# Log-softmax over 8192 rows: which 32 rows make up a tile, and what that does to the shape of its transfers

## The chip, the cores and the metric

The kernel runs on one core of a Trainium2 chip. The metric is device microseconds (us) of one execution. Three runs of the kernel before took 7587.55, 7586.4 and 7587.37 us, median 7587.37 us.

## The reference

The input is float32 of shape 16 x 512 x 50000, that is 8192 rows of 50,000 numbers (200,000 bytes a row, 1638.4 MB in all). The output has the same shape.

```python
max_x = np.max(x, axis=-1, keepdims=True)
shifted = x - max_x
log_sum_exp = np.log(np.sum(np.exp(shifted), axis=-1, keepdims=True))
return (shifted - log_sum_exp).astype(np.float32)
```

Each row is independent of every other one, so the rows may be taken in any order and any grouping.

## The kernel before, in words

**Tiles.** A tile is 32 rows (`R`). Each row is cut into four parts (`G`), so that a tile fills 128 partitions with 12,500 numbers (50,000 bytes) each. There are 256 tiles (`ntiles`) and four buffers (`NBUF`), and tile t lives in buffer t modulo 4. A buffer is loaded, worked on in place and stored; then it is loaded again.

**Which rows.** `halves` (L77 to L79) views the array as two halves of 128 tiles. Tile t is tile t // 2 of half t % 2, so that even tiles come from the first 4096 rows and odd ones from the last 4096. The 32 rows of a tile are neighbours in memory: the 128 partitions read 128 neighbouring stretches of 50,000 bytes. `run` (L85 to L94) gives the same tiles to the loops, where the tile number is in a register.

**The first tile** is taken in four pieces (`NS`), so that work starts as soon as a quarter of it is there. A piece is eight whole rows, each cut into 16 parts (`GS`) of 3,125 numbers (12,500 bytes), one to a partition. `xs` and `os` (L82, L83) are the views for it. Pieces are loaded at L173 and stored from `in_parts` of the scalar engine through L278. The last tile is stored in four pieces too, but these are quarters of the columns of an ordinary tile (L334).

**Engines.** SP issues the loads (L170 whole tiles, L173 the pieces of the first tile); before a buffer is loaded again, SP waits until its store has landed (`take`, L49). ACT issues the stores (L278). The two queues are called q10 and q1 in the profile. DVE takes the maxima of four column blocks of a tile (L231), agrees them among the four partitions of a row, and at the end subtracts maximum and logarithm in place over the whole tile (L219). ACT takes the exponentials (L286) as the maxima come, and the logarithm (L274). PE adds up the partial sums of a row with a small matmul (L340). ACT issues the store of tile t - 1 when it is half through the exponentials of tile t (`GATE`).

**Order.** Everything is written out by hand with semaphores: SP loads pieces 0 to 3 of tile 0, then tiles 1, 2, 3, and then each further tile as soon as the store of the tile four before it has landed. A loop of 63 rounds of four tiles makes up the middle.

Of the kernel before, what the change touches and what calls it, by code (L numbers as in the profile page):

```python
# [16 lines left out]
G = 4  # L17
R = P // G
C = 3125
NBUF = 4  # L20

NS = 4

GATE = 2
GS = G * NS
RS = P // GS
# [20 lines left out]
def take(engine, sem, n=16):  # L47

    engine.wait_ge(sem, n).then_inc(sem, -n)  # L49


def cols(c):
    return slice(c * C, (c + 1) * C)
# [3 lines left out]
def kernel(  # L57
# [6 lines left out]
    xf = x.flatten_outer_dims()  # L64
    of = out.flatten_outer_dims()
# [3 lines left out]
    ntiles = N // R  # L69


    rounds = (ntiles - NBUF) // NBUF
# [1 line left out]
    tail = range(1 + rounds * NBUF, ntiles)  # L74


    def halves(a):  # L77
        both = a.rearrange("(h t r) (g w) -> h t (r g) w", h=2, r=R, g=G)
        return [both[t % 2, t // 2] for t in range(ntiles)], both  # L79

    (xt, xh), (ot, oh) = halves(xf), halves(of)
    xs = xf.rearrange("(t s r) (g w) -> t s (r g) w", s=NS, r=RS, g=GS)  # L82
    os = of.rearrange("(t s r) (g w) -> t s (r g) w", s=NS, r=RS, g=GS)  # L83

    def run(both, first, n):  # L85

        k = NBUF // 2

        def tile_of(q, i):
            h, t = (first + i) % 2, (first + i) // 2  # L90
            part = both[h, t : t + k * (n - 1) + 1 : k]
            return part[bass.ds(q, 1)].rearrange("o p w -> (o p) w")

        return tile_of  # L94

    data = ctx.enter_context(tc.tile_pool(name="data", bufs=1))
    stats = ctx.enter_context(tc.tile_pool(name="stats", bufs=1))
# [10 lines left out]
    bufs = [data.tile([P, W], FP32, name=f"buf{j}") for j in range(NBUF)]  # L108
# [41 lines left out]
    @block.gpsimd  # L150
    def _(gpsimd):
        k = 0
        for g in (GS, G):
            view = ones[g].rearrange("p (r g) -> p r g", g=g)
            r = P // g
            gpsimd.memset(ones[g], 1.0).then_inc(ready)
            gpsimd.affine_select(  # L157
                out=view, in_=view, pattern=[[-g, r], [0, g]], base=0,
                channel_multiplier=1, compare_op=ALU.is_ge, fill=0.0,
            ).wait_op(ready, k + 1, "sem-ge").then_inc(ready)  # L160
            gpsimd.affine_select(  # L161
                out=view, in_=view, pattern=[[g, r], [0, g]], base=g - 1,
                channel_multiplier=-1, compare_op=ALU.is_ge, fill=0.0,
            ).wait_op(ready, k + 2, "sem-ge").then_inc(ready)
            k += 3

    @block.sync
    def _(sync):
        def load(j, src):
            sync.dma_start(out=bufs[j], in_=src).then_inc(landed[j], 16)  # L170

        for s in range(NS):
            sync.dma_start(out=bufs[0][:, cols(s)], in_=xs[0, s]).then_inc(  # L173
                landed_part[s], 16
            )
        for t in range(1, NBUF):
            load(t, xt[t])
        take(sync, stored[0], 16 * NS)
        load(0, xt[NBUF])
        src = run(xh, NBUF + 1, rounds - 1)  # L180
        with sync.Fori(0, rounds - 1) as q:
            for i in range(NBUF):
                j = (i + 1) % NBUF
                take(sync, stored[j])
                load(j, src(q, i))
        for t in tail:
            take(sync, stored[t % NBUF])
            load(t % NBUF, xt[t])
        for j in range(NBUF - 1):
            take(sync, stored[j])  # L190
        take(sync, stored[NBUF - 1], 16 * NS)
# [78 lines left out]
    @block.scalar  # L270
    def _(scalar):
        def log(k):
            added.next(
                scalar.activation(out=logs[k], in_=rowsums[k], func=ACT.Ln)  # L274
            ).then_inc(logged.sem)

        def store(j, dst, buf):
            subtracted.next(scalar.dma_start(out=dst, in_=buf)).then_inc(stored[j], 16)  # L278

        def whole(j, dst=None):  # L280

            for c in range(NS):
                if c == GATE and dst is not None:
                    store((j - 1) % NBUF, dst, bufs[(j - 1) % NBUF])
                shifted.next(
                    scalar.activation(  # L286
                        out=dump, in_=bufs[j][:, cols(c)], func=ACT.Exp,
                        bias=negms[j][:, c : c + 1], scale=1.0,
                        accum_out=parts[j][:, c : c + 1],
                    )  # L290
                ).then_inc(on_act.sem)
                on_act.next(scalar.nop())  # L292
            agreed.next(
                scalar.activation(  # L294
                    out=scales[j], in_=negms[j], func=ACT.Exp,
                    bias=negmaxs[j][:, 0:1], scale=-1.0,
                )
            ).then_inc(rescaled.sem)
            log(j)

        def in_parts(j, t):
            for s in range(NS):
                agreed.next(
                    scalar.activation(  # L304
                        out=dump, in_=bufs[j][:, cols(s)], func=ACT.Exp,
                        bias=negmaxs[NBUF + s][:, 0:1], scale=1.0,
                        accum_out=sub_sum[:, s : s + 1],
                    )
                ).then_inc(summed_part.sem)
                if s:  # L310
                    store(j, os[t, s - 1], bufs[j][:, cols(s - 1)])
                log(NBUF + s)
            store(j, os[t, NS - 1], bufs[j][:, cols(NS - 1)])

        def settle():
            for count in (on_act, shifted, agreed, added, subtracted):
                count.settle(scalar)

        nc.scalar.preload_act_table_set("natural_log_exp_and_others")  # L319
        in_parts(0, 0)  # L320
        settle()
        whole(1)
        settle()
        dst = run(oh, 1, rounds)
        with scalar.Fori(0, rounds) as q:
            for i in range(NBUF):
                whole((i + 2) % NBUF, dst(q, i))
            settle()
        for t in tail[1:-1]:
            whole(t % NBUF, ot[t - 1])  # L330
        store(t % NBUF, ot[t], bufs[t % NBUF])
        whole(NBUF - 1)
        for c in range(NS):
            store(NBUF - 1, ot[ntiles - 1][:, cols(c)], bufs[NBUF - 1][:, cols(c)])  # L334

    @block.tensor
    def _(tensor):
# [58 lines left out]
```

## Time and profile before

| | |
|---|---|
| median of three runs | 7587.37 us |
| the profiled execution | 7587.55 us |
| its span in the profile | 7585.8 us |
| bytes moved | 1638.40 MB read, 1638.40 MB written, 432 GB/s over the span |
| DVE busy | 5443.9 us (72%) |
| ACT busy | 3184.9 us (42%) |
| PE busy | 478.3 us (6%) |

The span is the time from the first to the last instruction that the profile shows on the core; 1.75 us of the profiled execution lie outside it. A page of the profile has the busy time of each engine, the span cut into 40 equal slices (the DMA line gives tenths of the time in which the 16 DMA engines were busy, the GB/s line what they moved), the DMA queues with their packets, the groups of instructions, and the transfers with the time from issue to landing. Further views give waits, a timeline, and sums for chosen stretches.

### The profile page before, as it was taken

To read this page: it belongs to the slowest core of one execution; us is meant where nothing else is said; L and a number is where in the kernel's file an instruction comes from. 1 tells how busy PE (TensorE), PEld (TensorE's weight loads), DVE (VectorE), ACT (ScalarE), POOL (GpSimd) and SP (SyncE) were. 2 spreads that over 40 slices of the span, in tenths; PEclk is the share of its full clock that TensorE was granted. 3 is DMA by queue.
4 is the path that set the end of the run, shared out by engine and by line. 5 is a ranking of instruction groups with operands and counts; after the bars stand their busy time and mean duration, and the time that the engine had idled before them with its cause. 6 is when DMAs were issued, how large, how long until landed. Compare 5 with 4: busy or idle time off the path is not lost. (4 is left out here: it accounts for less than half of the span.)

```text
span 7585.8 us, 13839 instructions
## 1 busy us (share of the span) xinstructions
PE 478.3 (6%) x2048; PEld 456.1 (6%) x2048; DVE 5443.9 (72%) x2832; ACT 3184.9 (42%) x2563; POOL 2.3 (0%) x10
## 2 busy tenths in 40 slices
PE   0000000000000000000000000000000000000000
PEld 0000000000000000000000000000000000000000
DVE  7777777777777777777777777777777777777776
ACT  4344443444434434444443444434444343444433
POOL 0000000000000000000000000000000000000000
DMA  9999999999999999999999999999999999999999
GB/s 424 431 434 434 434 434 433 432 434 434 434 434 433 433 433 432 434 432 433 432 433 434 432 433 433 432 434 431 434 434 431 434 432 433 433 432 434 432 433 398
DMA packets 75026, 3276.85 MB, mean 432 GB/s; under 512 B 8336, under 2 KB 8336, under 8 KB 8336
## 3 DMA queue, kind: packets, MB, share of 16 engines
q1 hardware_dynamic: 37296, 1638.42, 50.0%
q10 hardware_dynamic: 37728, 1638.42, 50.0%
q14 instruction: 2, 0.02, 0.0%
HBM read 1638.40 MB, written 1638.40 MB: 432 GB/s over the span
## 5 line engine op out<-in xcount | busy, mean ns | idle before, releaser
L286 ACT ACTIVATE dump<-buf,negm 128x3125 f32<-128x3125 f32 x1020 | 2925.8, 2868 | 3787.0 <-DVE negm L231 3748.7
L231 DVE TENSOR_REDUCE negm<-buf 128x1 f32<-128x3125 f32 x1020 | 3405.1, 3401 | 912.1 <-DVEq L49 912.1
L219 DVE TENSOR_SCALAR buf<-buf,negmax,logsum 128x12500 f32<-128x12500 f32 (+1 forms) x262 | 1739.6, 6641 | 553.9 <-ACT logsum L274 553.9
L340 PE MATMUL sums<-scaled,ones 128*128 128x1 f32 x2040 | 476.0, 355 | 7054.5 <-DVE scaled L242 7054.5
L340 PEld LDWEIGHTS sums<-scaled,ones 128*128 128x128 f32 x2040 | 454.1, 327 | 7076.3 <-DVE scaled L242 7076.3
L242 DVE TENSOR_TENSOR scaled<-scale,part 128x4 f32<-128x4 f32 x255 | 41.4, 162 | 577.6 <-ACT scale L294 577.6
L274 ACT ACTIVATE logsum<-sums 128x1 f32<-128x1 f32 x259 | 44.4, 171 | 551.7 <-PE sums L340 549.0
L286 ACT ACTIVATION_READ_ACCUMULATOR dump<-buf,negm 128x1 f32 x1020 | 190.0, 186 | 0.0
L294 ACT ACTIVATE scale<-negm,negmax 128x4 f32<-128x4 f32 x255 | 75.8, 297 | 23.5
L236 DVE TENSOR_REDUCE negp<-negm 128x1 f32<-128x4 f32 x255 | 40.0, 157 | 39.0 <-DVE negm L231 39.0
L214 DVE STREAM_TRANSPOSE negmax<-spread 128x32 f32<-128x32 f32 x259 | 54.9, 212 | 9.0
L198 DVE STREAM_TRANSPOSE allneg<-negp 128x32 f32<-128x32 f32 x259 | 54.8, 212 | 9.0
L201 DVE TENSOR_REDUCE rowneg<-allneg 128x8 f32<-128x32 f32 (+1 forms) x259 | 48.2, 186 | 9.0
L208 DVE COPY spread<-rowneg 128x32 f32<-128x32 f32 x259 | 47.0, 182 | 9.0
L249 DVE TENSOR_REDUCE negp<-buf 128x1 f32<-128x3125 f32 x4 | 13.6, 3402 | 7.5 <-DVEq L49 7.5
L304 ACT ACTIVATE dump<-buf,negmax 128x3125 f32<-128x3125 f32 x4 | 11.5, 2868 | 14.4 <-DVE negmax L214 14.4
L351 PE MATMUL sums<-sub_sum,ones 128*128 128x1 f32 x8 | 2.3, 362 | 29.5 <-ACT dump L304 29.5
L351 PEld LDWEIGHTS sums<-sub_sum,ones 128*128 128x128 f32 x8 | 2.0, 310 | 29.8 <-ACT dump L304 29.8
L319 ACT ACT_TABLE_LOAD x1 | 1.3, 1283 | 1.0 <-SPq L128 1.0
L157 POOL TENSOR_SCALAR_AFFINE_SELECT ones<-ones 128x128 f32<-128x128 f32 x2 | 0.9, 441 | 0.1
L161 POOL TENSOR_SCALAR_AFFINE_SELECT ones<-ones 128x128 f32<-128x128 f32 x2 | 0.9, 427 | 0.1
L304 ACT ACTIVATION_READ_ACCUMULATOR dump<-buf,negmax 128x1 f32 x4 | 0.7, 186 | 0.0
(5 smaller groups left out, 0.8 us busy)
## 6 DMA issues: line engine op xcount, KB each, us to landing
buf<-in_x_dram SPq DMA_DIRECT2D x255, 6250.0 KB, 36.7
out_dram<-buf ACTq DMA_DIRECT2D x254, 6250.0 KB, 41.7
out_dram<-buf ACTq DMA_DIRECT2D x8, 1562.5 KB, 19.0
buf<-in_x_dram SPq DMA_DIRECT2D x4, 1562.5 KB, 11.3
```

Source lines behind the costliest of these rows:

```text
L198: vector.transpose(out=allneg, in_=negp.to_broadcast([P, SQ]))
L201: vector.tensor_reduce(out=rowneg[:, : SQ // g], in_=allneg.rearrange("p (r g) -> p r g", g=g), op=op, axis=AX, negate=negate,)
L208: vector.tensor_copy(out=spread.rearrange("p (r g) -> p r g", g=g), in_=rowneg[:, : SQ // g, None].to_broadcast([P, SQ // g, g]),)
L214: vector.transpose(out=negmaxs[k], in_=spread)
L219: ins = vector.tensor_scalar(out=buf, in0=buf, scalar1=negmaxs[k][:, 0:1], scalar2=logs[k], op0=ALU.add, op1=ALU.subtract,)
L231: vector.tensor_reduce(out=negms[j][:, c : c + 1], in_=bufs[j][:, cols(c)], op=ALU.max, axis=AX, negate=True,).then_inc(shifted.sem if c < ...
L236: vector.tensor_reduce(out=negp, in_=negms[j], op=ALU.min, axis=AX).then_inc(on_dve.sem)
L242: vector.tensor_mul(out=scaleds[j], in0=scales[j], in1=parts[j])
L274: scalar.activation(out=logs[k], in_=rowsums[k], func=ACT.Ln)
L286: scalar.activation(out=dump, in_=bufs[j][:, cols(c)], func=ACT.Exp, bias=negms[j][:, c : c + 1], scale=1.0, accum_out=parts[j][:, c : c + 1],
L294: scalar.activation(out=scales[j], in_=negms[j], func=ACT.Exp, bias=negmaxs[j][:, 0:1], scale=-1.0,)
L340: ins = tensor.matmul(rowsums[j], ones[G], scaleds[j][:, c : c + 1], start=c == 0, stop=c == NS - 1,)
```

## The change

Tile t now takes row t, row 256 + t, row 512 + t and so on: one row of each of 32 stretches of 256 rows. The four parts of one row are still neighbours in memory, but the next row of the tile lies 256 rows (51.2 MB) further. From tile to tile, every address moves on by one row. The first tile (tile 0) consists of rows 0, 256, 512, ...; a piece of it is eight of these rows, each in 16 parts. The views that are handed to the transfers have one dimension more.

```diff
-    def halves(a):
-        both = a.rearrange("(h t r) (g w) -> h t (r g) w", h=2, r=R, g=G)
-        return [both[t % 2, t // 2] for t in range(ntiles)], both
-
-    (xt, xh), (ot, oh) = halves(xf), halves(of)
-    xs = xf.rearrange("(t s r) (g w) -> t s (r g) w", s=NS, r=RS, g=GS)
-    os = of.rearrange("(t s r) (g w) -> t s (r g) w", s=NS, r=RS, g=GS)
-
-    def run(both, first, n):
-
-        k = NBUF // 2
-
-        def tile_of(q, i):
-            h, t = (first + i) % 2, (first + i) // 2
-            part = both[h, t : t + k * (n - 1) + 1 : k]
-            return part[bass.ds(q, 1)].rearrange("o p w -> (o p) w")
-
-        return tile_of
+    xt = xf.rearrange("(r t) (g w) -> t r g w", r=R, g=G)
+    ot = of.rearrange("(r t) (g w) -> t r g w", r=R, g=G)
+    xs = xf.rearrange("(s r t) (g w) -> t s r g w", s=NS, r=RS, g=GS)
+    os = of.rearrange("(s r t) (g w) -> t s r g w", s=NS, r=RS, g=GS)
+
+    def run(a, first, n):
+
+        part = a[first : first + NBUF * n].rearrange("(q i) r g w -> q i r g w", i=NBUF)
+        return lambda q, i: part[bass.ds(q, 1), i].rearrange("o r g w -> (o r) g w")
...
-        src = run(xh, NBUF + 1, rounds - 1)
+        src = run(xt, NBUF + 1, rounds - 1)
...
-        dst = run(oh, 1, rounds)
+        dst = run(ot, 1, rounds)
...
-            store(NBUF - 1, ot[ntiles - 1][:, cols(c)], bufs[NBUF - 1][:, cols(c)])
+            store(NBUF - 1, ot[ntiles - 1][:, :, cols(c)], bufs[NBUF - 1][:, cols(c)])
```

In the built program, the DRAM side of each transfer is written down as a list of counts, the slowest first. It changes as follows; the buffer side counts 128 partitions in all of them, before and after.

| transfer | before | after |
|---|---|---|
| whole tile | 128 x 12500 | 32 x 4 x 12500 |
| piece of the first tile | 128 x 3125 | 8 x 16 x 3125 |
| piece of the last tile | 128 x 3125 | 32 x 4 x 3125 |

The order of the instructions on all engines, and their number, are the same in both programs.

## The prediction

> **What bounds the kernel now.** I read the page's slices first, then its DMA queues, then its transfers, then SP's waits.
>
> ```profile
> DMA  9999999999999999999999999999999999999999
> GB/s 424 431 434 434 434 434 433 432 434 434 434 434 433 433 433 432 434 432 433 432 433 434 432 433 433 432 434 431 434 434 431 434 432 433 433 432 434 432 433 398
> DMA packets 75026, 3276.85 MB, mean 432 GB/s; under 512 B 8336, under 2 KB 8336, under 8 KB 8336
> ...
> q1 hardware_dynamic: 37296, 1638.42, 50.0%
> q10 hardware_dynamic: 37728, 1638.42, 50.0%
> ...
> buf<-in_x_dram SPq DMA_DIRECT2D x255, 6250.0 KB, 36.7
> out_dram<-buf ACTq DMA_DIRECT2D x254, 6250.0 KB, 41.7
> out_dram<-buf ACTq DMA_DIRECT2D x8, 1562.5 KB, 19.0
> buf<-in_x_dram SPq DMA_DIRECT2D x4, 1562.5 KB, 11.3
> ```
>
> The reader is to see one thing: the packets of the two queues fill 50.0% + 50.0% of 16 engines' span. No DMA engine has time left; DVE (72%) and ACT (42%) have. So a microsecond of work added to the busiest DMA engine is a microsecond of span, and nothing that happens on the other engines matters unless a DMA engine runs dry for it. The view of waits for SP's own queue says the same: a load is not late, it waits for a buffer whose store is still moving.
>
> ```profile
> SPq L49 <- SPq L49: 7429.6, 256, 74.0
> ```
>
> **Packets.** q1 has 37,296 packets for 255 + 4 loads, which is 144 a transfer; q10 has 37,728 for 254 + 8 stores, also 144. That is 128 (one a partition) and 16 small ones: 521 transfers x 16 = 8336, the count under 512 B. I read the small ones as one for each engine that takes part, at the end of its share; then every transfer is now spread over 16 engines, 8 partitions each. An engine's pace: 1638.42 MB in half of 16 x 7585.8 us (60,686 us) is 27.0 KB per us. A packet of 50,000 B takes 1.852 us, one of 12,500 B 0.463 us. One engine's span: (255 + 254) x 8 x 1.852 = 7541.4, and 12 pieces x 8 x 0.463 = 44.4, together 7585.8 us. The sum closes, as it must at 100%.
>
> **The change part by part.**
>
> *Whole tiles.* The DRAM side counts 32 x 4 where it counted 128. 32 rows split evenly over 16 engines, two rows or 8 packets of 50,000 B each, as now. The number, size and spread of packets stay, so 0 us from the shape.
>
> *Where these packets lie in DRAM.* Rows of a tile are 51.2 MB apart instead of 200 KB. No row of this trace has such a distance, so I bound it by the slices. The order of before already walks through all of both arrays, and its 38 inner slices lie between 431 and 434 GB/s, mean 433.0. Were all at 434, the 7205 us of the inner slices would be 17 us shorter; were all at 431, 33 us longer. I take 0, because the pace hardly depends on where a slice lies. Ends kept: -17 and +33 us.
>
> [...]
>
> *The pieces of the first tile.* Here I expect the time to go. A piece's DRAM side counts 8 x 16 where it counted 128. If a transfer is divided along that slowest count, 16 engines no longer divide it: eight rows go to eight engines, 16 packets of 12,500 B each, and the other eight engines get none. There are 4 loads and 4 stores of such pieces. Busy engines: 8 x 16 = 128 packets instead of 64, so 64 x 0.463 = +29.6 us at the pace of now. Idle ones: 29.6 us less, which helps nobody, since a tile is ready only when all its engines have landed, and buffers come free only then.
>
> Can it hide? Beside it lies only the work of the same engines, which are full to the end, so no. Nor do they run dry at the start, which would add to it. After 2 us of issue they hold 59.3 us of pieces in and out and 3 x 8 x 1.852 = 44.4 us of tiles 1 to 3, work until 105.7 us. Tile 1 lands there by 2 + 29.6 + 14.8 + at most half of the piece stores (14.8) = 61 us. In the timeline its store is issued 36 us after its landing (73.48 against 37.66), here at 97 us, 9 us before the work ends. What DVE and ACT do later at the start is covered by these 44.4 us; if that cover were gone, their delay of some 10 us would come on top.
>
> What does one piece packet cost in this new spread? [...] The trace has no such row. Lower bound: the pace of now, factor 1, from the queue rows. Upper bound: the largest ratio of landing to bare moving that any row has, the stores, 41.7 us against 6.4 MB at 16 x 27.0 = 14.8 us, factor 2.8. (The factor is that of two queues sharing 16 engines plus the wait in line; it is borrowed.) Whole loads have 36.7 / 14.8 = 2.5. Nearest in kind is two parties at one path, which is factor 2, between these rows. The busy engines then spend 128 x 0.926 = 118.5 us on pieces instead of 29.6: **+88.9 us**. At factor 1 it is +29.6, at 2.8 it is 165.9 - 29.6 = +136.3.
>
> [...]
>
> *Issue.* The three-count transfers may take SP and ACT longer to issue: now 0.34 us on ACT, 0.55 on SP (four in 2.19). Even at twice that, 262 stores add 89 us to ACT's 3184.9, and its slack of 4400 us hides them; a store that is issued 0.3 us later finds its engines busy with others. 0 us. If the engines were dry, it would be up to 0.9 us in each of 256 tiles.
>
> *Pieces of the last tile.* 32 x 4 x 3125: 16 engines as now, 0 us. Instructions on all engines, and the loops, are the same in number and order.
>
> **Sum.** 7587.55 (the profiled execution, 0.18 above the median of the runs) + 88.9 = 7676.4 us.
>
> **The rivals.**
>
> *Eight engines at the pace of now.* +29.6, so 7617.2 us. For it: all packets of before have the same pace, whatever partition they go to. [...]
>
> *The pieces still run on 16 engines.* 128 partitions on the other side can be divided by 16, and a row's 16 parts too. Then nothing is added: 7587.6 us, no change. It decides if the packet counts stay at 144 in all 521 transfers. This is the rival on the other side.
>
> *Distance in DRAM slows every packet.* Then each per cent of packet time is 76 us, and from 0.2% it can be told. [...] Against it: the even slices.
>
> *Distance in DRAM helps.* At 434 throughout, and the pieces costing nothing, 7587.6 - 17 = 7571 us. Against it: there are only 17 us to win.
>
> **How the numbers follow.** Forecast (eight engines, packets slowed by meeting) 0.52; eight engines at the pace of now 0.28; 16 engines still 0.10; distance slows 0.07; distance helps 0.03. The predicted time is the first one's, 7676. The range takes in its bounds and the first rival, with 5 us of play below: 7612 to 7724; the last three cases, 0.20, are left out. About 0.2% (15 us) is what a measurement of this kernel can tell from no change: faster 0.03, same 0.10, slower 0.87.
>
> **What would show it.** Small packets 8336 - 8 x 8 = 8272, and 74,962 packets in all; if it is 8336, the step of the eight engines is wrong. The first slice falls: 88.9 us less of some 433 GB/s in 189.6 us gives about 220 instead of 424 GB/s (about 356 at +29.6), while the inner slices stay at 431 to 434; if these move, the DRAM step is wrong. DVE's first wait, 7.5 us now, grows to about 11 at the pace of now, to 18 and more at factor 2. SP's first loads after tile 3 come later by the whole difference of the span; if they come later by more, it was made up afterwards.

## The result, and the profile after

The changed kernel took 7666.8 us in the median (7662.31 to 7670.28, four runs) against 7587.46 us before: a ratio of 1.0105, 95% interval 1.0087 to 1.0122, so 79 us slower. The profiled execution took 7670.28 us with a span of 7668.6 us, 82.7 us more than the one of before. In the packet counts below, q1 carries the loads and q10 the stores. On the chips of the experiments some executions, of the kernel before too, took some 60 to 180 us (one 370) longer than the others of their kernel; the times below are medians of the others, called undisturbed, while the ratios and their intervals compare averages that count some of the longer ones as well.

The page of the kernel after, its slices, DMA queues and transfers:

```profile
DMA  8999999999999999999999999999999999999999
GB/s 246 431 432 434 434 433 431 433 434 432 433 433 432 432 434 433 431 433 433 431 433 433 433 432 434 433 431 433 434 431 433 433 433 432 433 433 432 433 434 402
DMA packets 74962, 3276.85 MB, mean 427 GB/s; under 512 B 8272, under 2 KB 8272, under 8 KB 8272
...
q1 hardware_dynamic: 37264, 1638.42, 50.1%
q10 hardware_dynamic: 37696, 1638.42, 49.6%
...
buf<-in_x_dram SPq DMA_DIRECT2D x255, 6250.0 KB, 36.8
out_dram<-buf ACTq DMA_DIRECT2D x254, 6250.0 KB, 41.7
```

Of the 40 slices only the first has changed clearly: 246 where it was 424. The inner slices (431 to 434) and the transfers of whole tiles are as before. 64 small packets are gone, eight for each of the eight pieces of tile 0, so each piece ran on eight engines. The landings say the same: the first piece had 16 of them in the kernel before and has eight now, between 22.2 and 23.6 us.

The same in stretches of 100 us. The columns after the stretch are the busy times of PE, its weight loads, DVE, ACT and POOL with their instructions, then the clock, the busy share of the DMA engines and the GB/s. Before:

```profile
0.00:100.00 100.00, 6.07 (x24) 5.56 (x24) 76.70 (x50) 45.06 (x38) 2.29 (x10) 1.00 0.99 415
100.00:200.00 100.00, 7.47 (x32) 7.13 (x32) 74.34 (x41) 43.48 (x36) 0.00 (x0) 1.00 1.00 431
```

and after:

```profile
0.00:100.00 100.00, 2.34 (x8) 2.00 (x8) 24.07 (x24) 13.94 (x13) 2.29 (x10) 1.00 0.98 207
100.00:200.00 100.00, 5.59 (x24) 5.34 (x24) 63.58 (x33) 37.30 (x30) 0.00 (x0) 1.00 0.76 300
```

These four lines hold two different losses. In the first 100 us the engines are as busy as before (0.98 against 0.99) and move half as much: their packets are slow. In the second 100 us the share is 0.76: some engines have nothing to do and wait for the others, since a buffer is free only when all engines have landed. Together 33.9 MB less are moved in 200 us; at 433 GB/s that is 78 us.

The first maxima of DVE on the pieces (L249 before, L240 after) show when the pieces of tile 0 are there. Start, duration, then what the engine waited for; the first and the last of before, and the four after:

```profile
7.51 3.41 DVE L249 TENSOR_REDUCE negp<-buf 128x1 f32<-128x3125 f32 x1 [7.51 <-DVEq L49]
...
23.84 3.40 DVE L249 TENSOR_REDUCE negp<-buf 128x1 f32<-128x3125 f32 x1
```

```profile
23.71 3.41 DVE L240 TENSOR_REDUCE negp<-buf 128x1 f32<-128x3125 f32 x1 [23.71 <-DVEq L49]
44.81 3.41 DVE L240 TENSOR_REDUCE negp<-buf 128x1 f32<-128x3125 f32 x1 [16.77 <-DVEq L49]
66.06 3.41 DVE L240 TENSOR_REDUCE negp<-buf 128x1 f32<-128x3125 f32 x1 [15.12 <-DVEq L49]
89.42 3.41 DVE L240 TENSOR_REDUCE negp<-buf 128x1 f32<-128x3125 f32 x1 [17.23 <-DVEq L49]
```

Before, a piece landed some 3.7 us after the one ahead of it, the last at 18.6 us, and only the first maximum waited. Now a piece arrives every 21 to 23 us. SP's eighth load, tile 4, waits for the store of tile 0. In SP's queue, before and after:

```profile
78.81 58.02 SPq L170 DMA_DIRECT2D buf<-in_x_dram  x3
```

```profile
165.28 57.63 SPq L161 DMA_DIRECT2D buf<-in_x_dram  x3
```

It is issued 86.5 us later than before; the load of tile 97 is 83 us later, and the last load of all 82.7. So the whole loss stands after 165 us, and at most some 4 us of it are made up in the 7500 us that follow.

The packet records of the traces give the mean time of one 12,500 B packet of tile 0: loads 1.114 us after, 0.485 before; stores 0.653 after, 0.468 before.

### The profile page after: what moved, and what is told of

It reads as the page before. It is cut to its first block, busy times and chain, and to the rows that moved or that the text cites. A ratio compares the mean times of both kernels' runs of the same rounds, so it can differ in the third digit from the quotient of the medians.

```text
span 7668.6 us, 13839 instructions
## 1 busy us (share of the span) xinstructions
PE 478.4 (6%) x2048; PEld 456.2 (6%) x2048; DVE 5444.4 (71%) x2832; ACT 3184.9 (42%) x2563; POOL 2.3 (0%) x10
## 2 busy tenths in 40 slices
DMA packets 74962, 3276.85 MB, mean 427 GB/s; under 512 B 8272, under 2 KB 8272, under 8 KB 8272
## 5 line engine op out<-in xcount | busy, mean ns | idle before, releaser
L285 ACT ACTIVATE scale<-negm,negmax 128x4 f32<-128x4 f32 x255 | 75.8, 297 | 23.6
L240 DVE TENSOR_REDUCE negp<-buf 128x1 f32<-128x3125 f32 x4 | 13.6, 3408 | 72.8 <-DVEq L49 72.8
## 6 DMA issues: line engine op xcount, KB each, us to landing
buf<-in_x_dram SPq DMA_DIRECT2D x255, 6250.0 KB, 36.8
out_dram<-buf ACTq DMA_DIRECT2D x254, 6250.0 KB, 41.7
```

The source lines that it names most:

```text
L285: scalar.activation(out=scales[j], in_=negms[j], func=ACT.Exp, bias=negmaxs[j][:, 0:1], scale=-1.0,)
```

## The experiments

The theory: all of the loss comes from the eight transfers of tile 0's pieces; they run on eight engines, and their packets are slow because engines meet, that is, slow one another while they work at the buffers at the same time. The meeting is my estimate: the packet records of the traces name neither engine nor partition, so it can only be inferred from how long packets take. The rivals: the distance of the rows in DRAM; the imbalance of eight engines at the usual packet pace; eight engines being slow by themselves.

**The changed kernel with tile 0 whole** (`e6_first_tile_whole`).

```diff
-        for s in range(NS):
-            sync.dma_start(out=bufs[0][:, cols(s)], in_=xs[0, s]).then_inc(
-                landed_part[s], 16
-            )
+        load(0, xt[0])
...
-        in_parts(0)
+        whole(0)
```

> The changed kernel, but tile 0 is loaded, worked on and stored as one whole tile (32 x 4 x 12500), like all others; all rows keep their far places. Theory 'pieces' (all of the loss comes from the four piece loads and stores of tile 0): no loss left, 7587 us within 15, small packets 16 in every transfer. Rival 'distance' (rows 51.2 MB apart cost something in every tile): the loss stays in part or whole, 7610 to 7667 us.

Measured: 7593.2 us (11 of 12 runs) against 7587.8 before on the same chip (22 of 29); ratio 0.9977, interval 0.9941 to 1.0013. Of the 79 us at most 5 are left, though every row is still 51.2 MB from the next of its tile. Its slices:

```profile
GB/s 416 433 433 433 434 434 434 434 433 434 432 432 434 434 432 433 434 432 433 433 431 434 433 431 434 431 433 434 431 433 434 431 433 434 431 434 433 431 434 398
```

The inner slices lie between 431 and 434, as in the kernel before and the changed one. Distance costs nothing that these runs can tell.

**Only the pieces undone** (`e1_far_tiles_flat_pieces`).

```diff
...
+    def far(a):
+        return a[R:].rearrange("(r t) (g w) -> t r g w", r=R, g=G)
+
+    def near(a):
+        return a[:R].rearrange("(t s r) (g w) -> t s (r g) w", t=1, s=NS, r=RS, g=GS)
```

> Undoes the pieces alone: tile 0 is the 32 neighbouring rows at the start of the array, its pieces are flat 128 x 3125 transfers again; tiles 1 to 255 take one row of each of 32 stretches of 255 rows, 51.0 MB apart, in the shape 32 x 4 x 12500. Theory 'pieces': no loss, 7587 us within 15, first slice at 424 GB/s again. Rival 'distance': 7610 to 7667 us.

Measured: six of seven undisturbed runs at 7567.9 to 7570.8 us and one at 7590.3; before, on the same chip, five of 24 at 7567 to 7568 and 19 at 7585 to 7590. Ratio 1.0009, interval 0.9970 to 1.0047. Its slices:

```profile
GB/s 423 432 434 432 435 432 435 433 434 434 432 435 433 434 435 432 435 433 434 435 432 435 433 434 435 433 435 433 434 435 433 435 433 434 435 433 434 433 433 414
```

The first is 423, as before the change. There is no loss; of the two levels, 7567 and 7587, more below.

**Only the pieces done** (`e2_near_tiles_row_pieces`), in the kernel before:

```diff
...
+    xs, os = (
+        a[E:H].rearrange("(s r o) (g w) -> o s r g w", o=2, s=NS, r=RS, g=GS)
+        for a in (xf, of)
+    )
```

> Does the pieces alone: the kernel before, tiles of 32 neighbouring rows in turns from the two halves, but tile 0 takes every second row of a block of 64 and tile 254 the other rows of it, so that the pieces have the shape 8 x 16 x 3125 with rows only 0.4 MB apart. Theory 'pieces, packets slowed by meeting': the whole loss is there, 60 to 95 us over the kernel before, piece load packets of about 1.1 us on average as in the changed kernel. Rival 'distance' (also the distance of the rows of a piece): no loss. Rival 'imbalance alone': +30 us.

Measured: 7662.45 us (10 of 10), ratio 1.0095, interval 1.0069 to 1.0121; 75 us over the median of before. Its load packets take 1.086 us. The page has the same marks as that of the changed kernel:

```profile
GB/s 254 433 433 434 432 434 434 432 434 434 432 434 433 433 434 432 434 433 432 434 432 433 434 433 432 434 432 434 434 431 434 433 431 434 433 432 434 432 433 399
DMA packets 74962, 3276.85 MB, mean 428 GB/s; under 512 B 8272, under 2 KB 8272, under 8 KB 8272
```

With rows 0.4 MB apart instead of 51.2 MB the loss is the same. So the rows' distance is not the cause, neither for the tiles nor for the pieces; the shape of eight transfers out of 521 is what costs.

**The row pieces moved in the kernel with tile 0 whole** (`e5_row_pieces_moved_only`) **and bands of 32 partitions on the same eight engines** (`e4_bands_on_eight_engines`).

```diff
...
+            sync.dma_start(out=bufs[0][:, cols(s)], in_=xs[0, s]).then_inc(landed[0], 16)
...
```

```diff
...
+            sync.dma_start(out=bufs[0][32 * s : 32 * s + 32], in_=xt[0, 8 * s : 8 * s + 8]).then_inc(landed[0], 16)
...
```

> As the kernel with tile 0 whole, but tile 0 is moved by the four 8 x 16 x 3125 transfers of the changed kernel, in and out, and worked on only when all four are there. The parts of a row of tile 0 then stand at other partitions than the computation takes them for, so the output of these 32 rows is not the reference's. Theory 'pieces, packets slowed by meeting': the loss is back, 60 to 95 us over the kernel with tile 0 whole, piece load packets of about 1.2 to 1.4 us. Rival 'imbalance alone' (eight engines, each packet at its usual pace): +30 us. Rival 'distance': as the kernel with tile 0 whole.

> As the kernel with tile 0 whole, but tile 0 is moved by four transfers of 32 partitions each (8 x 4 x 12500): again eight engines carry all of tile 0, the same bytes each as with the 8 x 16 x 3125 pieces, but in packets of 50,000 B and to four neighbouring partitions an engine, so that the eight do not meet one another. Theory 'pieces, packets slowed by meeting': the imbalance stays (+30 us) and the meeting of the eight is gone; what may be left is a meeting with the engines that load tile 1 to 3 in half of the transfers, up to +15: so 25 to 50 us over the kernel with tile 0 whole, clearly less than with the 8 x 16 x 3125 pieces. Rival 'eight engines are slow by themselves' (whatever the partitions): the same 60 to 95 us.

Measured: 7669.5 us (10 of 10) with the row pieces, 76 us over the kernel with tile 0 whole, and 7638.5 us (only two of four) with the bands, 45 us over it. Both have 8272 small packets, so both move tile 0 on eight engines. The load packets of the row pieces take 1.258 us, although no engine computes on tile 0 before all of it is there; so the computation beside them is not what slows them. DVE's first maximum, when all of tile 0 is there, with the row pieces:

```profile
84.33 13.35 DVE L220 TENSOR_REDUCE negm<-buf 128x1 f32<-128x3125 f32 x4 [84.33 <-DVEq L49]
```

and with the bands:

```profile
50.84 13.35 DVE L220 TENSOR_REDUCE negm<-buf 128x1 f32<-128x3125 f32 x4 [50.84 <-DVEq L49]
```

The same bytes, of the same rows, on the same number of engines take 33 us less to come in as 8 x 4 x 12500 into 32 partitions a transfer than as 8 x 16 x 3125 into 128. The bands' packets are four times as long too, which is not separated here; but in the kernel before, packets of 12,500 B took 0.468 us, a quarter of the 1.847 us for 50,000 B, so short packets are not slow by themselves. Nor are eight engines: up to 18 us the 50,000 B load packets of the run with bands take 1.95 us in the mean. And imbalance alone, 30 us, is not all. What the bands have over 30 us fits meetings with the engines that load tiles 1 to 3: from 18 to 51 us half of the load packets take 3.91 us or more, 2.1 times 1.847.

**The loads of tiles 1 to 3 held back** (`e3_tiles_after_pieces`).

```diff
+        sync.wait_ge(go, 1)
         for t in range(1, NBUF):
             load(t, xt[t])
...
+                if s == NS - 1:
+                    vector.nop().then_inc(go)
```

> The changed kernel, but the loads of tiles 1, 2 and 3 are issued only when the last piece of tile 0 has landed, so that the eight engines of the pieces have the partitions' paths to themselves. It takes cover away, so its time tells little. Theory 'packets slowed by meeting', pairs among the eight and a third from the engines that load tiles 1 to 3: the third is gone, load packets at twice 0.463 us, pieces about 15 us apart instead of 21 us now, the first one there at about 19 instead of 23.7 us. Rival 'slow because of where the rows lie in DRAM': the pieces stay 21 us apart. Rival 'the eight engines meet only with the others, not with one another': pieces 7.5 us apart.

The arrival of its pieces:

```profile
17.81 3.41 DVE L244 TENSOR_REDUCE negp<-buf 128x1 f32<-128x3125 f32 x1 [17.81 <-DVEq L49]
31.39 3.41 DVE L244 TENSOR_REDUCE negp<-buf 128x1 f32<-128x3125 f32 x1 [9.24 <-DVEq L49]
44.89 3.41 DVE L244 TENSOR_REDUCE negp<-buf 128x1 f32<-128x3125 f32 x1 [7.38 <-DVEq L49]
59.88 3.41 DVE L244 TENSOR_REDUCE negp<-buf 128x1 f32<-128x3125 f32 x1 [8.86 <-DVEq L49]
```

They come 13.5 to 15.0 us apart, against 21 to 23 us with the other loads beside them and 7.4 us at the usual pace (16 packets of 0.463 us). Load packets take 0.751 us in the mean, 1.6 times 0.463; their 75th and 90th percentiles are 0.91 and 0.93, twice 0.463. In the changed kernel these percentiles are 1.40 and 1.43, three times. So the loads of tiles 1 to 3 do slow the pieces, and the eight still slow one another; the factors 2 and 3 fit meetings in pairs, with the engines of tiles 1 to 3 as a third. The time, 7631 to 7677 us in seven of eight runs, is hardly worse anywhere than that of the changed kernel, although eight engines stand idle for 60 us: holding the loads back saved 22 us in the median of the seven, 39 in the profiled run.

**Two pieces of 16 rows** (`e7_two_pieces_sixteen_rows`).

```diff
-    xs = xf.rearrange("(s r t) (g w) -> t s r g w", s=NS, r=RS, g=GS)
+    xs = xf.rearrange("(s r t) (g w) -> t s r g w", s=NP, r=RS, g=GS)
```

with `NP = 2`, so `RS` is 16 and `GS` is 8.

> The changed kernel, but tile 0 in two pieces of 16 rows in 8 parts (16 x 8 x 6250) instead of four of 8 rows in 16 parts: the slowest count is 16 again, so all 16 engines take part, with the same bytes each. Rival 'imbalance alone': no loss, 7587 us within 15. Theory 'pieces, packets slowed by meeting': 16 engines with eight neighbouring partitions each still do not stand as in a whole tile and meet in pairs; packets of 25,000 B go at up to twice their 0.93 us, tile 0 takes 15 us longer in and up to 15 longer out: 7595 to 7620 us.

Measured: six undisturbed runs of 12, five at 7586.4 to 7587.8 us and one at 7604.5; ratio 1.0011, interval 0.9962 to 1.0059. By its time alone this is the rival's run, and my range was missed. The profile shows more:

```profile
GB/s 383 434 434 434 434 434 433 434 433 434 434 434 433 434 433 434 434 434 434 434 433 434 434 433 433 434 434 434 434 433 434 434 434 434 434 434 434 433 434 413
...
buf<-in_x_dram SPq DMA_DIRECT2D x2, 3125.0 KB, 25.8
```

The first slice is down to 383, which is 18 us of moving, and the 25,000 B load packets take 1.902 us, 2.05 times 0.926 (the stores 1.070). All 16 engines take part (8272 small packets are 16 in each of 517 transfers), with the same bytes each if each takes the eight packets of one row, and still the loads go at half pace, as if the engines met in pairs. In this execution the loss does not show in the time, since it ran without the slow engine that the profiled run of before has (last section): its inner slices are at 433 and 434 and the last at 413. Beside the profile of only the pieces undone, which ran without it too (span 7569.1, first slice 423), its span of 7585.6 is 16.5 us longer. Whether the other runs at 7587 us lacked that engine too is not shown.

**Loads and stores apart** (`e8_row_loads_flat_stores`, `e9_flat_loads_row_stores`): only one side of tile 0 in the 8 x 16 x 3125 shape.

```diff
...
+    xs, os = (
+        a[E : E + R].rearrange("(t s r) (g w) -> t s (r g) w", t=1, s=NS, r=RS, g=GS)
+        if a is of
+        else a[E:H].rearrange("(s r o) (g w) -> o s r g w", o=2, s=NS, r=RS, g=GS)
+        for a in (xf, of)
+    )
```

(`a is xf` in the second.)

> The pieces alone, in the loads alone: as the kernel with near tiles and row pieces (8 x 16 x 3125, rows 0.4 MB apart), but tile 0 is stored in flat 128 x 3125 pieces on 16 engines; the results of tile 0 and 254 (64 rows) are then written to other rows of the same block, so these rows of the output are not the reference's. Theory 'packets slowed by meeting': the load packets alone meet the engines of tiles 1 to 3, so most of the loss is here: 64 load packets of some 1.2 us instead of 32 of 0.47, +45 to 65 us over the kernel before. Rival 'imbalance alone': half of 30 us, +15.

> The pieces alone, in the stores alone: tile 0 and 254 are loaded flat on 16 engines, and tile 0 is stored in 8 x 16 x 3125 pieces; again 64 rows of the output stand at other rows of their block. Theory 'packets slowed by meeting': stores have only one another to meet, and do so only in part of the time, since each engine sends a load packet between two of them: 64 store packets at 0.47 to 0.93 us instead of 32 at 0.47, +15 to +30 us over the kernel before, less than the loads alone. Rival 'loads and stores weigh the same': half of the loss, +40.

Measured: 7649.0 us with the loads (10 of 10; ratio 1.0066, interval 1.0031 to 1.0102) and 7611.3 us with the stores (10 of 10; 1.0029, 0.9997 to 1.0061). The undisturbed runs of before on that chip are four at 7567 to 7571 and seven at 7583 to 7591 us. Over the median of those seven, 7587.9, the loads cost 61 us and the stores 23, together 84, where both at once cost 75 to 79; over the lower level it is 20 us more each. By its interval alone the cost of the stores cannot be told from nothing. The packets of the row loads take 1.157 us, those of the row stores 0.605. First slices 287 and 371:

```profile
GB/s 287 432 435 434 432 435 432 434 435 432 435 434 430 432 433 432 432 431 435 432 435 431 435 432 434 432 434 433 432 434 432 435 432 435 431 434 432 435 432 403
```

```profile
GB/s 371 430 434 433 433 433 433 433 434 432 434 433 433 433 433 433 433 433 433 433 433 432 433 433 433 433 433 433 431 434 433 432 433 432 432 433 432 434 433 404
```

Set against the 424 of before, the bytes that these first slices lack are 60 and 23 us at 433 GB/s; the same sum gives 79 us for the changed kernel. Loads and stores do not weigh the same.

## Why the prediction was right, point by point

- **What bounds.** Right: the DMA engines are full, with a busy share of 1.00 from 200 to 7400 us. Tile 4 is loaded 86.5 us late and the last load 82.7 us late, so a delay of the first 165 us is not regained, but for some 4 us.
- **Whole tiles, shape.** Right, it costs 0 us: their transfers land in 36.8 and 41.7 us, as before, and the kernel with tile 0 whole has at most 5 us of loss.
- **Distance in DRAM.** I took 0 us, and that was right: the inner slices stayed at 431 to 434 with the rows of a tile 51.2 MB apart, and lay at 432 to 435 with 51.0 MB (only the pieces undone). No other distance of this size was tried.
- **Eight engines.** Right, and to the packet: 8272 and 74,962. That a transfer is divided along its slowest count was my estimate, which nothing in the trace of before showed. The runs bear it out for 8 (eight landings for the first piece), for 16 (two pieces of 16 rows, 16 small packets in each of 517 transfers) and for 32 (16 in each of the 513 transfers of the changed kernel that are not pieces of tile 0).
- **Factor of a piece packet.** That packets would be slowed was right; that the sum came out so close was partly luck, since I took factor 2 for loads and stores alike. No run shows a factor 2 for both; it was an estimate between 1 and 2.8. Loads had 1.114 / 0.463 = 2.4, stores 0.653 / 0.463 = 1.4. The eight engines' mean, 64 x 1.114 + 64 x 0.653 = 113.1 us, is 82.6 us over the 30.5 us of before; the forecast was 88.9. The mis-sized terms lie on both sides of 2. The engines of tile 1 as a third party, which I had not put into the sum, are real and large: a quarter of the load packets take 1.40 us or more, factor 3, and with those engines held back the mean falls from 1.114 to 0.751 us. That stores are slowed less I did not see; that it is because a load packet stands between any two of them fits the run with row stores alone, but is not shown. Nor does any run show which partitions an engine serves, or where engines meet; the runs show the slowing (1.114 us in the changed kernel, 1.902 for the 25,000 B of the two pieces) and what takes it away. The mean over the eight also hides that they do not end together: the loads of each piece land within 1.3 to 2.3 us, but the eight landings of the last piece's store spread from 152.9 to 165.2 us, and tile 4 waits for the last of them.
- **Cover at the start.** It was right that the busy engines have work throughout, and wrong that tiles 1 to 3 were only cover. They also slowed the pieces, and were slowed: their load packets of the first 150 us take 2.92 us in the mean instead of 1.89. With these loads held back, the pieces came 13.5 to 15.0 us apart instead of 21 to 23.
- **Issue.** SP now takes 0.70 us for one of the first four loads (0.55 before), ACT 0.55 to 0.64 a store (0.34 to 0.38) and 1.21 for the first. One issue, SP's of tile 3, took 8.33 us (7.7 to 8.1 in the three other runs with row-piece loads beside those of tiles 1 to 3), more than the doubling that I had allowed for. The engines had other loads in hand, so I still put the issue at 0 us, as forecast, though no run tests it alone.
- **Signs.** The first slice is 246, forecast 220 (356 without meeting); DVE's first wait is 23.7 us, forecast 18 and more; SP's first load after tile 3 comes 86.5 us later, against 82.7 in the span, so a little was made up.

## What to carry to other kernels

Where the DMA engines are full from end to end, the balance among them counts even in a few transfers: eight transfers out of 521 cost 1%, because one set of engines got more work, or slower packets, in the first 165 us and never had a pause in which to catch up. When rows are regrouped, look at the slowest count on the DRAM side of each transfer and not only at bytes and contiguous runs: 32 x 4 cost nothing, 8 x 16 halved the engines and made load packets 2.4 times as long, and 16 x 8 kept all 16 engines but made them 2.05 times as long. Read the busy share beside the GB/s: here a high share with few GB/s (0.98 and 207) was slow packets, and a low share (0.76) was engines that waited for others.

## What the runs showed that I had not expected

The kernel before has two undisturbed levels, about 7567 us (5 of 24 runs on one chip) and about 7587. In the trace of before, the 16 landings of a whole load lie within 2.9 us up to 1100 us of the span; then one engine drops behind the other fifteen, 0.9 us at 1443, 3.2 at 2509, 12.4 at 2870 and 15.4 at 3580, and stays there to the end. In the profiled run of only the pieces undone (span 7569.1), no landing of these loads lies more than 5.3 us behind the one ahead of it, the inner slices reach 435 and the last slice is 414 instead of 398. This fits a cost of some 20 us for a single engine that falls behind, as an imbalance that is not regained; in runs without a trace it is not shown. In the changed kernel four engines land last together, 7 to 9 us behind the other twelve up to 500 us of the span and 11 to 15 us from about 1100 us on. The first slices, which end at 190 us, are not touched by any engine that drops behind later. Why an engine falls behind is not shown, nor whether the order of the rows has a part in how often; six of seven undisturbed runs at the lower level with only the pieces undone, against five of 24, are too few to say, so no version is shown to beat the kernel before.
